# A transformer layer: the order of values and sums, more sevens in feed-forward 1, and gated results turned by transposing transfers

## The chip, the core and the metric

The kernel runs on one core of a Trainium2 chip. A core has a matrix engine (TensorE, PE in the profile; its weight loads are PEld), a vector engine (VectorE, DVE), a scalar engine (ScalarE, ACT), GpSimd (POOL) and a queue engine (SyncE, SP). Each runs its own instructions in order and waits for the others by semaphores. TensorE writes to PSUM, eight banks of 128 x 512 words; everything else lies in SBUF or in HBM. Transfers are issued from SP's or ScalarE's queue and are carried by 16 DMA engines. The metric is the device time of one execution in microseconds; less is better.

## The reference

One layer over 256 tokens of width 2048, in float32: a half feed-forward (SwiGLU, 5632 wide), two token mixers side by side (retention and sliding-window attention), a second half feed-forward, a gated input embedding, with a layer norm after each.

```python
def swiglu(x, w_gu, w_down):
    g, u = jnp.split(x @ w_gu, 2, axis=-1)
    return (jax.nn.silu(g) * u) @ w_down
...
h = layer_norm(alpha * h + 0.5 * swiglu(h, w_ffn1_gu[i], w_ffn1_down[i]), ln_g[i, 0], ln_b[i, 0])
rq, rk, rv, rg, aq, ak, av, gate_r, gate_a = jnp.split(h @ w_in[i], SPLIT_POINTS, axis=-1)
...
h = layer_norm(alpha * h + mixed, ln_g[i, 1], ln_b[i, 1])
h = layer_norm(alpha * h + 0.5 * swiglu(h, w_ffn2_gu[i], w_ffn2_down[i]), ln_g[i, 2], ln_b[i, 2])
```

The weights are random normal numbers, all different, so nothing can be left out.

## The kernel before

**Three matmuls for one.** A float32 product is made of parts in a format that TensorE takes at full pace: each operand is split into a high part (a cast on ScalarE, line 98) and a low part (a subtraction on VectorE, line 99), and three of the four products are added up (lines 374 to 376). Every weight is split on the way in, so each 512 KB chunk of weights costs a ScalarE cast and a VectorE subtraction of 128 x 1024 elements.

**Plain units and sevens.** Weight chunks come in pairs: two contraction blocks of 128 by two column blocks, against two blocks of 128 tokens. A plain unit ("P") multiplies all eight products, 24 matmuls, and needs two casts and two subtractions. A seven ("S", class `Seven`) has seven products (21 matmuls) after Strassen and Winograd; VectorE makes four sums of the weights for it (t1 to t4, lines 170 to 173, in tiles u and v), and ScalarE and VectorE split three more tiles. Its products go into the usual sums and into four banks of their own, which `seven_common` folds after the last seven of a block (lines 479 to 483). A "D" (`Prepared`) is a seven whose sums were made earlier, during the mixers, by `sums_ahead`, put away in HBM and loaded back.

**Feed-forward.** `ffn` runs 11 gate-up blocks (512 columns of gate and of up at a time), each a list of units from `gu_units`: block 0 all plain; in feed-forward 1 then "PPSPSPSP" in odd blocks and "PPSSPSSP" in even ones; in feed-forward 2 blocks 1 to 5 and 7 hold D units besides. After a block VectorE adds the sums (line 970), ScalarE takes Silu (line 971), VectorE multiplies (line 972), and the result v is turned (tokens by features to features by tokens) by eight transposes of 128 x 128 on TensorE into two banks and two copies on ScalarE (`turned`, lines 905 to 916). The down projection follows, in two halves.

**Order by hand.** Nothing is reordered: each engine's program is the order in which the Python code calls it. `plan` lists all weight units in the order of use. After each unit, `done` calls `fill`, which makes further units (casts, sums, subtractions) while those made ahead hold less than `ahead` matmul times (45; a plain chunk counts 12, a seven 21) and loads further ones while less than `far` (90) is under way and the slots suffice (`slots_for_weights`; 46 slots of 4 KB per partition in all). Then `run_side` runs one job of the list `side`; `later(n, job)` puts a job behind n others. It also takes a step of `lazy`, where `sums_ahead` and the rotary tables wait. PSUM banks and slots are handed out at the first write, those free longest first.

In steady state a gate-up block "PPSSPSSP" gives this order of making: first the next seven, then (after two units) the second seven, two plain chunks, the third and the fourth seven, four plain chunks, then the fold. `turned` runs behind the third chunk of the next block, that is between the second seven's casts and the next plain chunk's cast on ScalarE.

**The value projection.** `mixers` starts with the value block 0 (plain, its first part interleaved with the norm before), then splits it and makes the token forms that sevens need (`forms_of`), then runs value blocks 1 and 2 as one block of units "PSPSPSPS" (`VALUE_UNITS`, tiles rvsa, rvsb, rvss), then block 3 (plain, tile rv), then the rotary features (`features_out`, tile rqk).

Of the kernel before, what the change touches and what calls it, by code (L numbers as in the profile page):

```python
# [9 lines left out]
F32R = mybir.dt.float32r  # L10
I32 = mybir.dt.int32
AF = mybir.ActivationFunctionType
ALU = mybir.AluOpType
PSUM = bass.MemoryType.PSUM

P = 128
# [39 lines left out]
def layer(ctx: ExitStack, tc: tile.TileContext, io):  # L56
# [10 lines left out]
    def bank(name):  # L67
        return psum.tile([P, 512], F32, tag="ps", name=name)
# [4 lines left out]
    def slot(shape, dt, name):  # L73
        return slots.tile(shape, dt, tag="slot", name=name)
# [72 lines left out]
    class Seven:  # L147
# [12 lines left out]
        def make(self):  # L160
            a, b = self.a, self.b
            nm = a.name
            b11, b21, b12, b22 = a.of(a.raw, 0), a.of(a.raw, 1), b.of(b.raw, 0), b.of(b.raw, 1)
            u, v = (slot([P, 2, 512], F32, w + nm) for w in "uv")

            def shaped(x):
                return x.rearrange("p (g n) -> p g n", g=2) if a.paired else x

            t1, t3, t2, t4 = (shaped(x) for x in (u[:, 0], u[:, 1], v[:, 0], v[:, 1]))
            dve.tensor_tensor(t1, b11, b12, ALU.add)  # L170
            dve.tensor_tensor(t3, b12, b22, ALU.add)  # L171
            dve.tensor_tensor(t2, b11, t3, ALU.add)
            dve.tensor_tensor(t4, t2, b21, ALU.add)  # L173

            def parted(name, x):
                hi, lo = (slot([P, 2, 512], F32R, w + name + nm) for w in "hl")
                split(hi, lo, x)
                return [(hi[:, e], lo[:, e]) for e in range(2)]

            a.make()  # L180
            self.b11, self.b21 = a.columns(0), a.columns(1)
            both = slot([P, 2, 512], F32R, "b" + nm)
            self.b22 = both[:, 0], both[:, 1]
            split(shaped(both[:, 0]), shaped(both[:, 1]), b22)
            self.t1, self.t3 = parted("u", u)
            self.t2, self.t4 = parted("v", v)

# [215 lines left out]

    def block(name, units, keys, lhs, forms, sums, fold, before=None):


        sevens = [p for kind, p in units if kind != "P"]
        if sevens:
            p1, p6, p7, q5 = (Sum(bank(f"{name}s{j}"), len(sevens)) for j in range(4))
        for j, (kind, p) in enumerate(units):  # L410
# [24 lines left out]
            if p == sevens[-1]:  # L435
                fold(p1.ap, p6.ap, p7.ap, q5.ap)

    def seven_forms(full, hi, lo):
# [457 lines left out]
    def ffn(name, i, ht, norm, keep, residual, keepers, away):  # L896
# [9 lines left out]
        def turned(j, v):  # L906

            raw = slot([P, 4, S], F32, f"{name}a{j}")
            raws.append(raw)
            ps = banks(f"{name}t{j}")  # L910
            for k in range(4):
                for t in range(2):
                    at = slice(k % 2 * S + t * P, k % 2 * S + t * P + P)
                    pe.transpose(ps[k // 2][:, at], v[:, t, k * P : (k + 1) * P], ident)
            for h in range(2):
                act.copy(raw[:, 2 * h : 2 * h + 2], ps[h].rearrange("p (b n) -> p b n", b=2))

# [6 lines left out]

        for j in range(KF // 4):
            pg, pu = banks(f"{name}g{j}"), banks(f"{name}u{j}")
            units = gu_units(name, j)
# [36 lines left out]

            block(f"{name}{j}", units, gu_keys(name, j), rhs, forms, sums, lambda *a: got.extend(seven_common(*a)), before)
            if got:
# [148 lines left out]
    def mixers(ht, norm, residual, keepers, away):  # L1115
# [8 lines left out]

        rv = []
        made = {}
# [12 lines left out]
        def values(blk, ps):  # L1139
            hi, lo = (slot([P, 2, 512], F32R, f"rv{w}{blk}") for w in "hl")  # L1140
            if isinstance(ps, list):
                for t in range(2):
                    split(hi[:, t], lo[:, t], ps[t])
            else:
                split(hi, lo, ps)
            rv.append((hi, lo))

# [656 lines left out]
```

## Time and profile before

| | |
|---|---|
| three runs, median (lowest to highest) | 2283.04 us (2282.73 to 2283.24) |
| span of the profiled execution | 2282.8 us |
| feed-forward 1, ten gate-up blocks from turn to turn | 420.4 us |
| feed-forward 2, the same | 413.6 us |
| granted TensorE clock, mean | 0.996 |
| HBM read, written | 484.43 MB, 29.36 MB |

The span runs from the first to the last instruction of one profiled execution; it agrees with the runs. In views of instructions in order of time, a row gives start, duration, engine, line of the code, operation, output<-input and shapes, and in square brackets the idle time ahead of it with what ended it. VectorE's and ScalarE's instructions overlap a little, so the step from one start to the next is what an operation costs its engine. "PE 42.38 (x193)" in a stretch means busy time and number of instructions.

### The profile page before, as it was taken

To read this page: it belongs to the slowest core of one execution; us is meant where nothing else is said; L and a number is where in the kernel's file an instruction comes from. 1 tells how busy PE (TensorE), PEld (TensorE's weight loads), DVE (VectorE), ACT (ScalarE), POOL (GpSimd) and SP (SyncE) were. 2 spreads that over 40 slices of the span, in tenths; PEclk is the share of its full clock that TensorE was granted. 3 is DMA by queue.
4 is the path that set the end of the run, shared out by engine and by line. 5 is a ranking of instruction groups with operands and counts; after the bars stand their busy time and mean duration, and the time that the engine had idled before them with its cause. 6 is when DMAs were issued, how large, how long until landed. Compare 5 with 4: busy or idle time off the path is not lost.

```text
span 2282.8 us, 29225 instructions
## 1 busy us (share of the span) xinstructions
PE 2265.0 (99%) x10485; PEld 1881.8 (82%) x10485; DVE 2025.6 (89%) x2628; ACT 1233.5 (54%) x1502; POOL 2.3 (0%) x9
## 2 busy tenths in 40 slices
PE   9999999999999899999999999999999999999999
PEld 7888888888887788888778888888888888888887
DVE  7999999999989989888789788789999999889887
ACT  6555555556554545445565545455555565655543
POOL 0000000000000000000000000000000000000000
PEclk9999999999999899999999999999999999999999
DMA  8666665665677679876446658886867766555872
GB/s 300 208 199 200 198 208 180 207 198 183 228 278 255 220 251 298 283 231 213 152 143 202 225 179 290 305 287 223 291 240 255 263 203 207 199 186 211 290 272 74
DMA packets 211129, 515.72 MB, mean 226 GB/s; under 512 B 16412, under 2 KB 20892, under 8 KB 210984
## 3 DMA queue, kind: packets, MB, share of 16 engines
q1 hardware_dynamic: 209000, 511.28, 66.2%
q10 hardware_dynamic: 1984, 2.58, 0.4%
q8 instruction: 82, 1.34, 0.2%
q14 instruction: 63, 0.52, 0.1%
HBM read 484.43 MB, written 29.36 MB: 225 GB/s over the span
## 4 chain that ended last, share of the span: by engine, by line
PE 97%; DVE 1%; DMA 1%; ACT 0%; issue 0%; ACTq 0%; SPq 0%; DVEq 0%
PE f1g L374 3%; PE f1g L376 3%; PE f1g L375 3%; PE f2g L376 3%; PE f2g L375 3%; PE f2g L374 3%; PE rqk L325 3%; PE f1u L374 2%; PE f1u L375 2%; PE f1u L376 2%; PE f2u L375 2%; PE f2u L376 2%; PE f2u L374 2%; PE aqk L325 2%; PE f2d L374 2%; PE f1d L376 2%
## 5 line engine op out<-in xcount | busy, mean ns | idle before, releaser
L99 DVE TENSOR_TENSOR lf_gu<-rf_gu,hf_gu 128x1024 fp32r<-128x1024 f32 (+1 forms) x274 | 323.2, 1211 | 13.9 <-ACT hf_gu L98 12.8
L98 ACT CAST hf_gu<-rf_gu 128x1024 fp32r<-128x1024 f32 (+1 forms) x274 | 273.9, 1043 | 29.9 <-DMA rf_gu<-in_f_gu 27.5
L99 DVE TENSOR_TENSOR lf_down<-rf_down,hf_down 128x1024 fp32r<-128x1024 f32 x150 | 178.7, 1220 | 16.8 <-ACT hf_down L98 16.3
L99 DVE TENSOR_TENSOR lw_in_f<-rw_in_f,hw_in_f 128x1024 fp32r<-128x1024 f32 x140 | 167.6, 1220 | 24.7 <-ACT hw_in_f L98 24.6
L98 ACT CAST hf_down<-rf_down 128x1024 fp32r<-128x1024 f32 x150 | 151.7, 1050 | 48.7 <-DMA rf_down<-in_f_down 20.4
L98 ACT CAST huf_gu<-uf_gu 128x1024 fp32r<-128x1024 f32 x70 | 73.8, 1054 | 145.6 <-DVE uf_gu L171 135.1
L98 ACT CAST hw_in_f<-rw_in_f 128x1024 fp32r<-128x1024 f32 x140 | 140.6, 1050 | 8.7 <-PE rqk L333 2.3
L374 PE MATMUL f1g<-hf_gu,xt 128*128 128x512 f32 x247 | 96.4, 390 | 0.5 <-ACT hf_gu L98 0.5
L376 PE MATMUL f1g<-lf_gu,xt 128*128 128x512 f32 x247 | 96.5, 391 | 0.0
L375 PE MATMUL f1g<-hf_gu,xt 128*128 128x512 f32 x247 | 96.2, 389 | 0.0
L98 ACT CAST hvf_gu<-vf_gu 128x1024 fp32r<-128x1024 f32 x70 | 73.8, 1054 | 29.5 <-DVE vf_gu L173 29.0
L971 ACT ACTIVATE eve<-eve 128x1024 f32<-128x1024 f32 x20 | 21.2, 1062 | 126.7 <-DVE eve L970 126.7
L99 DVE TENSOR_TENSOR luf_gu<-uf_gu,huf_gu 128x1024 fp32r<-128x1024 f32 x70 | 85.3, 1219 | 0.0
L99 DVE TENSOR_TENSOR lvf_gu<-vf_gu,hvf_gu 128x1024 fp32r<-128x1024 f32 x70 | 85.3, 1219 | 0.0
L374 PE MATMUL f2g<-hf_gu,ht 128*128 128x512 f32 x217 | 84.7, 390 | 0.0
L376 PE MATMUL f2g<-lf_gu,ht 128*128 128x512 f32 x217 | 84.7, 390 | 0.0
L375 PE MATMUL f2g<-hf_gu,ht 128*128 128x512 f32 x217 | 84.5, 389 | 0.0
L374 PE MATMUL f1u<-hf_gu,xt 128*128 128x512 f32 x212 | 83.4, 394 | 0.0
L375 PE MATMUL f1u<-hf_gu,xt 128*128 128x512 f32 x212 | 82.6, 390 | 0.0
L376 PE MATMUL f1u<-lf_gu,xt 128*128 128x512 f32 x212 | 82.6, 390 | 0.0
L374 PE MATMUL f2u<-hf_gu,ht 128*128 128x512 f32 x172 | 68.2, 397 | 0.0
L376 PE MATMUL f2u<-lf_gu,ht 128*128 128x512 f32 x172 | 67.1, 390 | 0.0
(1562 smaller groups left out, 6606.4 us busy)
## 6 DMA issues: line engine op xcount, KB each, us to landing
rf_gu<-in_f_gu SPq DMA_DIRECT2D x360, 512.0 KB
rf_down<-in_f_down SPq DMA_DIRECT2D x176, 512.0 KB
rw_in_f<-in_w_in_f SPq DMA_DIRECT2D x148, 512.0 KB
rw_rv<-in_w_rv SPq DMA_DIRECT2D x32, 512.0 KB
rw_ret<-in_w_ret SPq DMA_DIRECT2D x32, 512.0 KB
rw_mix<-in_w_mix SPq DMA_DIRECT2D x32, 512.0 KB
rw_pg<-in_w_pg SPq DMA_DIRECT2D x32, 512.0 KB
rw_att<-in_w_att SPq DMA_DIRECT2D x16, 512.0 KB
```

The costliest lines, as they stand in the source:

```text
L98: act.copy(dst_hi, src)
L99: (lo_engine or dve).tensor_tensor(dst_lo, src, dst_hi, ALU.subtract)
L325: pe.matmul(ps[f], hi[:, kk, f * P : (f + 1) * P], rhs(k), start=k == 0, stop=k == n_k - 1,)
L374: pe.matmul(o, al, bh, start=first, stop=False)
L375: pe.matmul(o, ah, bh, start=False, stop=False)
L376: pe.matmul(o, ah, bl, start=False, stop=self.left == 0)
L971: act.activation(g, g, AF.Silu)
```

## The change

Four things are edited. (1) In `Seven.make`, the order of the casts, sums and subtractions: sum three is made first, sum four after the low part of the first chunk; the work is the same. (2) In `mixers` and the plan, value block 3 comes before blocks 1 and 2. (3) `gu_units` gives every block without D units "PPSSPSSP": five more sevens in feed-forward 1 and one (block 9) in feed-forward 2. (4) `turned` no longer uses TensorE: ScalarE copies the upper and lower 16-bit halves of v into a tile `parts`, a transposing transfer of 16-bit words goes from ScalarE's queue to a tile `turns`, and three jobs later `join` copies the halves back together (two ScalarE copies). The product of gate and up is put off by one job, and from block 2 on, every other block names its four seven banks before its gate and up banks.

```diff
             t1, t3, t2, t4 = (shaped(x) for x in (u[:, 0], u[:, 1], v[:, 0], v[:, 1]))
+            a.make_hi()
...
+            act.copy(a.hi, a.raw)
+            act.copy(h22, b22)
+            dve.tensor_tensor(t3, b12, b22, ALU.add)
             dve.tensor_tensor(t1, b11, b12, ALU.add)
-            dve.tensor_tensor(t3, b12, b22, ALU.add)
             dve.tensor_tensor(t2, b11, t3, ALU.add)
+            act.copy(uh, u)
+            dve.tensor_tensor(a.lo, a.raw, a.hi, ALU.subtract)
             dve.tensor_tensor(t4, t2, b21, ALU.add)
...
+            act.copy(vh, v)
+            dve.tensor_tensor(l22, b22, h22, ALU.subtract)
+            dve.tensor_tensor(ul, u, uh, ALU.subtract)
+            dve.tensor_tensor(vl, v, vh, ALU.subtract)
...
-    def block(name, units, keys, lhs, forms, sums, fold, before=None):
+    def block(name, units, keys, lhs, forms, sums, fold, before=None, extra=None):
...
-            p1, p6, p7, q5 = (Sum(bank(f"{name}s{j}"), len(sevens)) for j in range(4))
+            p1, p6, p7, q5 = (Sum(b, len(sevens)) for b in extra or seven_banks(name))
...
-        order = "PPSSPSSP" if j % 2 == 0 else "PPSPSPSP"
-        return units_of(order, SEVEN[: order.count("S")])
+        return units_of("PPSSPSSP", SEVEN)
...
         def turned(j, v):
 
+            parts = slot([P, 2, 2, 512], U16, f"{name}w{j}")
+            words = v.bitcast(U16).rearrange("p t (n w) -> p w t n", w=2)
+            for w in range(2):
+                act.copy(parts[:, w], words[:, w])
+            turns = slot([P, 16, P], U16, f"{name}t{j}")
+            act.dma_start_transpose(turns, parts.rearrange("p w t n -> p (w t n)"))
+            later(3, lambda: join(j, turns))
+
+        def join(j, turns):
             raw = slot([P, 4, S], F32, f"{name}a{j}")
             raws.append(raw)
-            ps = banks(f"{name}t{j}")
-            for k in range(4):
-                for t in range(2):
-                    at = slice(k % 2 * S + t * P, k % 2 * S + t * P + P)
-                    pe.transpose(ps[k // 2][:, at], v[:, t, k * P : (k + 1) * P], ident)
-            for h in range(2):
-                act.copy(raw[:, 2 * h : 2 * h + 2], ps[h].rearrange("p (b n) -> p b n", b=2))
+            words = raw.bitcast(U16).rearrange("p k (t n w) -> p w k t n", t=2, w=2)
+            turns = turns.rearrange("p (w t k) n -> p w k t n", w=2, t=2)
+            for w in range(2):
+                act.copy(words[:, w], turns[:, w])
...
+            extra = seven_banks(f"{name}{j}") if j and j % 2 == 0 else None
             pg, pu = banks(f"{name}g{j}"), banks(f"{name}u{j}")
...
-                dve.tensor_tensor(v, g, v, ALU.mult)
+                later(1, lambda g=g, v=v: dve.tensor_tensor(v, g, v, ALU.mult))
...
         plan_tokens(("w_rv", 0), KD)
+        plan_tokens(("w_rv", 3), KD)
         block_units(VALUE_UNITS, value_keys)
-        plan_tokens(("w_rv", 3), KD)
...
+        ps = banks("rv3")
+        tokens_out(("w_rv", 3), KD, rhs, ps)
+        values(3, ps)
+        slots_for_weights(22)
         for n, v in enumerate(mixer_block("rvs", VALUE_UNITS, value_keys, rhs)):
             values(1 + n, v)
         made.clear()
         slots_for_weights(14)
-        ps = banks("rv3")
-        tokens_out(("w_rv", 3), KD, rhs, ps)
-        values(3, ps)
```

More of the change, by code (lines that the diff above doesn't have):

```diff
@@ L11 @@
 I32 = mybir.dt.int32
+U16 = mybir.dt.uint16
 AF = mybir.ActivationFunctionType
@@ L169, in make @@
             t1, t3, t2, t4 = (shaped(x) for x in (u[:, 0], u[:, 1], v[:, 0], v[:, 1]))
+            a.make_hi()
+            both = slot([P, 2, 512], F32R, "b" + nm)
+            h22, l22 = shaped(both[:, 0]), shaped(both[:, 1])
+            uh, ul, vh, vl = (slot([P, 2, 512], F32R, w + nm) for w in ("hu", "lu", "hv", "lv"))
+            act.copy(a.hi, a.raw)
+            act.copy(h22, b22)
+            dve.tensor_tensor(t3, b12, b22, ALU.add)
             dve.tensor_tensor(t1, b11, b12, ALU.add)
-            dve.tensor_tensor(t3, b12, b22, ALU.add)
             dve.tensor_tensor(t2, b11, t3, ALU.add)
+            act.copy(uh, u)
+            dve.tensor_tensor(a.lo, a.raw, a.hi, ALU.subtract)
             dve.tensor_tensor(t4, t2, b21, ALU.add)
[L175 to L180, printed above, removed]
+            act.copy(vh, v)
+            dve.tensor_tensor(l22, b22, h22, ALU.subtract)
+            dve.tensor_tensor(ul, u, uh, ALU.subtract)
+            dve.tensor_tensor(vl, v, vh, ALU.subtract)
             self.b11, self.b21 = a.columns(0), a.columns(1)
-            both = slot([P, 2, 512], F32R, "b" + nm)
             self.b22 = both[:, 0], both[:, 1]
-            split(shaped(both[:, 0]), shaped(both[:, 1]), b22)
-            self.t1, self.t3 = parted("u", u)
-            self.t2, self.t4 = parted("v", v)
+            self.t1, self.t3 = ((uh[:, e], ul[:, e]) for e in range(2))
+            self.t2, self.t4 = ((vh[:, e], vl[:, e]) for e in range(2))
     put_by_sums = {}
@@ L436, in block, with seven_banks @@
                 fold(p1.ap, p6.ap, p7.ap, q5.ap)
+    def seven_banks(name):
+        return [bank(f"{name}s{j}") for j in range(4)]
     def seven_forms(full, hi, lo):
@@ L963, in before @@
                     convert(u // 2 - 2)
-            block(f"{name}{j}", units, gu_keys(name, j), rhs, forms, sums, lambda *a: got.extend(seven_common(*a)), before)
+            block(f"{name}{j}", units, gu_keys(name, j), rhs, forms, sums, lambda *a: got.extend(seven_common(*a)), before, extra)
             if got:
@@ L1145, in values @@
                 split(hi, lo, ps)
[L1146 removed]
+            rv[blk] = hi, lo
         ps = banks("rv0")
```

2 lines of the change are left out of this document (1 added, 1 removed).

## The prediction

> **What bounds the kernel now.** I read the page first, then the stretches of the two gate-up loops, then who waits for whom, then VectorE's and ScalarE's instructions in order of time.
>
> ```profile
> span 2282.8 us, 29225 instructions
> PE 2265.0 (99%) x10485; PEld 1881.8 (82%) x10485; DVE 2025.6 (89%) x2628; ACT 1233.5 (54%) x1502; POOL 2.3 (0%) x9
> ```
>
> TensorE is idle for 17.8 us in all, so a gain must be matmul time taken away or one of its few waits. VectorE at 89% is close behind, which asks for a look at the stage.
>
> ```profile
> 58.25:100.63 42.38, 42.38 (x193) 35.19 (x192) 37.39 (x44) 23.43 (x27) 0.00 (x0) 1.00 0.69 222
> 100.63:142.33 41.70, 41.70 (x190) 34.64 (x189) 41.11 (x50) 23.98 (x27) 0.00 (x0) 1.00 0.60 191
> ...
> sum 420.40, PE 420.40 PEld 349.21 DVE 395.88 ACT 238.11 POOL 0.00; mean PE 42.04 PEld 34.92 DVE 39.59 ACT 23.81 POOL 0.00
> ```
>
> These stretches run from one turn of feed-forward 1 to the next (length; busy of PE, PEld, DVE, ACT, POOL; granted clock; DMA share; GB/s). The first is a block with three sevens, the second one with four, and so on in turn: ten blocks in 420.4 us, TensorE never idle. With four sevens VectorE is busy 41.11 of 41.70; only the blocks of three leave it 5 us. The ten like stretches of feed-forward 2:
>
> ```profile
> sum 413.60, PE 413.60 PEld 343.56 DVE 389.99 ACT 234.49 POOL 0.00; mean PE 41.36 PEld 34.36 DVE 39.00 ACT 23.45 POOL 0.00
> ```
>
> TensorE's long waits stand in the value projection:
>
> ```profile
> PE rvsa L374 <- DVE rvf0l L99: 6.5, 1, 6.5
> PE rv L374 <- DVE evw L480: 3.3, 1, 3.3
> ```
>
> **What TensorE saves.** From the chain of waits, the eight transposes of one turn:
>
> ```profile
> 58.25 0.87 PE f1t L914 x8
> ...
> 100.63 0.87 PE f1t L914 x8
> ```
>
> 22 turns of 0.87 make 19.1 us: twenty inside the stretches, two in the first down blocks (1.7 us). One seven in a pair of plain units' place is worth 42.38 - 41.70 = 0.68 us. Five more come in feed-forward 1 and one in block 9 of feed-forward 2 (its order is chosen by the same edited line): 6 x 0.68 = 4.1 us. A block of four sevens then needs 41.70 - 0.87 = **40.83 us** of TensorE, and an average block of feed-forward 1 now takes 42.04.
>
> **What VectorE's cycle becomes.** VectorE in block 2, where it has no gap:
>
> ```profile
> 101.10 0.69 DVE L170 TENSOR_TENSOR uf_gu<-rf_gu,rf_gu 128x512 f32<-128x512 f32 x1
> 101.70 0.69 DVE L171 TENSOR_TENSOR uf_gu<-rf_gu 128x512 f32<-128x512 f32 x1
> 102.42 0.69 DVE L172 TENSOR_TENSOR vf_gu<-rf_gu,uf_gu 128x512 f32<-128x512 f32 x1
> 103.15 0.69 DVE L173 TENSOR_TENSOR vf_gu<-vf_gu,rf_gu 128x512 f32<-128x512 f32 x1
> 103.76 1.22 DVE L99 TENSOR_TENSOR lf_gu<-rf_gu,hf_gu 128x1024 fp32r<-128x1024 f32 x1
> ...
> 106.63 1.22 DVE L99 TENSOR_TENSOR lvf_gu<-vf_gu,hvf_gu 128x1024 fp32r<-128x1024 f32 x1
> 107.77 2.35 DVE L99 TENSOR_TENSOR lf_gu<-rf_gu,hf_gu 128x1024 fp32r<-128x1024 f32 x2
> ...
> 130.10 0.68 DVE L483 TENSOR_TENSOR evw<-f12s,eve 128x512 f32<-128x512 f32 x1
> ...
> 142.21 1.22 DVE L99 TENSOR_TENSOR lvf_gu<-vf_gu,hvf_gu 128x1024 fp32r<-128x1024 f32 x1
> ```
>
> A seven takes eight operations, 101.10 to 107.77: 6.67 us. Its last one starts at 106.63; the same one three sevens, eight plain chunks and a fold later starts at 142.21. A block of four sevens thus costs VectorE 35.58 + 6.67 = **42.25 us**, against 41.70 on TensorE. It falls behind in such a block and catches up in the next.
>
> The new order inside a seven helps. An add that needs the result just before it starts 0.72 after it (101.70 to 102.42, 102.42 to 103.15), one that does not 0.61 (103.15 to 103.76). Sums one and three are swapped and a 1.13 us subtraction (106.63 to 107.77) stands ahead of the fourth sum, so both bubbles go: about 0.27 us a seven, 4 x 0.27 = 1.1 a block. Putting the product off by one unit saves the 0.1 to 0.2 us in which it waits for Silu. VectorE's cycle falls to about **41.0 us**. In the other stages' sevens the same 0.27 lies behind TensorE and is worth nothing.
>
> 41.0 against 40.83 would be a tie, if ScalarE were not in the way. Its instructions at the turn:
>
> ```profile
> 103.93 1.06 ACT L98 CAST hvf_gu<-vf_gu 128x1024 fp32r<-128x1024 f32 x1 [0.40 <-DVE vf_gu L173]
> 104.89 1.06 ACT L916 COPY f1a<-f1t 128x512 f32<-128x512 f32 x2
> 105.84 2.95 ACT L98 CAST hf_gu<-rf_gu 128x1024 fp32r<-128x1024 f32 x3
> ...
> 811.24 0.35 ACTq L818 DMA_DIRECT2D pos_ia<-in_positions  x1
> ```
>
> The turn stands between the casts of the second seven and the cast of the next plain chunk, and the first of those waits for the fourth sum on VectorE. Now the two copies (0.95 together) fit: the chunk's cast starts at 105.84 and is done at 106.9, 0.9 us before VectorE asks for it at 107.77. After the change ScalarE does there two copies of 1024 half words (I take 0.95 each, the step from 103.93 to 104.89), drains them, and issues the transfer. Counted from the fourth sum's end (3.69 us into the seven's 6.4): cast 1.05, copies 1.9, 0.2 for draining and semaphores, issue, chunk's cast 1.05. With the 0.35 us of a plain issue the cast is done at 8.3, and VectorE, ready at 6.4, stands still for 1.9 us. At the join two more copies (1.9) stand after the fourth seven's casts: done at 7.7, a stall of 1.3. Neither stall is made good, since VectorE has nothing left over: that such a cast can hold it shows already, in the rare cases where it comes late.
>
> ```profile
> DVE lf_gu L99 <- ACT hf_gu L98: 12.8, 18, 1.3
> ```
>
> The issue of a transposing transfer is in no row. Its lower bound is the 0.35 above; its upper bound is 16 of them, one for each 128 columns of the source: 5.6 us. It is one instruction on the same queue, so I go near the low end and take **1.0 us**. VectorE's cycle is then 41.0 + 1.9 + 1.3 + 0.65 = 44.85; I take **44.7 us**, since the drain may lie inside the issue.
>
> [...]
>
> Feed-forward 1: 10 x (44.7 - 40.83) = 38.7 us behind. Some is covered: the fold's last operation ended at 130.8 (row of 130.10), the next block's first matmul, which takes those banks, came 36 matmuls of 0.227 (0.68 / 3) before the turn at 142.33, at 134.2: 3.4 us, say 4 with what is made ahead. So 408.3 + 34.7 = 443 us, **+22.6**. Feed-forward 2 has cheaper blocks: where a prepared seven replaces one (1.73 us of VectorE for 6.4), the cycle is 39.5 us in three-seven blocks, 44.2 in the others, against 40.15 on TensorE. The short blocks and the cover of 4 take up most of what blocks 2, 4 and 6 lose; blocks 8 to 10 lose up to 3.9 each. I take 13 in all: 413.6 - 10 x 0.87 - 0.68 + 13 = 417.2, **+4**. So the gate-up loops lose more than TensorE saves in them. Each tenth of a us in the stall is worth 1.6 us of the time (ten blocks and some six).
>
> **The join's wait.** The join comes four units after the turn: two plain chunks and two sevens of VectorE's work, 2.3 + 12.8 = 15 us. A load of the same 512 KB took:
>
> ```profile
> 716.87 7.97 DMA rw_rv<-in_w_rv
> ```
>
> So I cost landing at nothing; beyond 15 us each us would hold ScalarE, and through it both engines, in every block. [...]
>
> **The values.** The first wait is real time, and more than itself:
>
> ```profile
> 746.18 0.80 PE L374 MATMUL rvsa<-bw_rv,rvf0l 128*128 128x512 f32 x1 [6.48 <-DVE rvf0l L99]
> ...
> 751.89 0.40 PE L375 MATMUL rvsb<-hvw_rv,ht 128*128 128x512 f32 x1
> ```
>
> Behind it 13 matmuls take 5.71 us, where 13 x 0.227 = 2.95 are due: TensorE runs at half pace at first. 6.5 + 2.8 = 9.3 us. Behind the second wait likewise: 3.3 + 2.8 = 6.1.
>
> ```profile
> 730.84 0.69 DVE L170 TENSOR_TENSOR uw_rv<-rw_rv,rw_rv 128x512 f32<-128x512 f32 x1
> ...
> 737.51 2.35 DVE L99 TENSOR_TENSOR lw_rv<-rw_rv,hw_rv 128x1024 fp32r<-128x1024 f32 x2
> ...
> 750.03 1.23 DVE L99 TENSOR_TENSOR rvf1l<-sums,rvf1h 128x1024 fp32r<-128x1024 f32 x1 [1.11 <-ACT rvf1h L98]
> ```
>
> With block 3 first, plain chunks are made from 730.84 on in place of a seven (6.67), the forms are done some 4 us earlier, about 747. The wait opened at 746.18 - 6.48 = 739.7, 30 matmuls after block 0's end, which was at 732.9. From there TensorE now has six of block 3's chunks, made by the planner's look-ahead, which last 16.3 us; it needs the seventh at 749.2. The first wait goes: **-9.3** (bounds 0, if a wait of its size opens there, and -15.4, if both go). The second I keep at its size: the fold of the sevens now stands before the first rotary features, VectorE's work up to it is the same but for 1 us, and the next features take the banks that the fold frees. The eight loads of block 3 move ahead of the sevens' on SP's queue; all have room there.
>
> **Edits at nothing.** Banks: the sums' banks came free 3.4 us before the next block used them, so their order changes nothing; were the gate's banks taken instead, each block would start 1 to 2 us late. Two more buffers per turn out of 46, and 0.5 MB per turn at a DMA share of 0.6 to 0.7: hidden behind loads that run ahead; without that cover the loads come late by the transfer's 2 to 8 us.
>
> **Sum**: +22.6 + 4 - 1.7 - 9.3 = +15.6 on the profiled 2282.8 (0.2 below the median of the runs): **2299 us**.
>
> **Rivals.** *TensorE stays the bound* (faster). If ScalarE's casts are not late, all savings stand: -19.1 - 4.1 - 9.3 = -32.5, **2250**. For it: VectorE's 41.0 ties with 40.83, and the averages leave VectorE 24.5 us in feed-forward 1. Against: those 24.5 lie in the three-seven blocks, which go. It is full where a block's stalls are nothing; by 1.6 us a tenth, the kernel is faster than before from stalls of 2.7 us downward (a cycle of 43.7), slower above. *ScalarE is held long by the issue*: at 2.8 us, eight plain issues, 1.8 more in some 16 bound blocks, +29: **2328**. For it: one instruction turns 16 column groups; against: the plain issue took a third of a us. [...] *Loss and gain cancel*, **2283**: at that cycle of 43.7, and a plain issue of 0.35 gives 44.0, which is near.
>
> **Chances.** Forecast 0.45 (its own range 2286 to 2318), TensorE-bound 0.27, long hold 0.20, cancelling 0.08. The range 2248 to 2338 leaves out the worst holds. A difference under 0.2% (4.6 us) can't be told from none: faster 0.28, within 0.09, slower 0.63.
>
> **What would show it.** Stretches of feed-forward 1 of 44 to 45 us with TensorE idle 3 to 4 us in each, and VectorE waiting for ScalarE's cast after the second and fourth seven; the first value wait gone, one before the rotary features. Stretches of 40.8 us would prove me wrong, ones beyond 46 the hold; waits of ScalarE for the transfer would show a late landing.

## The result, and the profile after

The changed kernel takes **2366.59 us** (median of 4 runs, 2364.87 to 2368.96) against 2282.99 us (2282.73 to 2283.24): a ratio of 1.0365, 95% interval 1.0353 to 1.0378. It is slower by 84 us. 2299 us was predicted, in a range up to 2338: the sign was right, and the loss is more than five times the 15.6 us forecast. Lines of the code behind `split` have moved: 99 and 100 are its cast and subtraction now, 175 to 186 the seven, 378 to 380 the matmuls, 917 to 928 the turn.

The page's head and its row of the queue that ScalarE issues on (packets, MB, share of the DMA engines), which held 1984 packets and 2.58 MB before:

```profile
span 2367.1 us, 28892 instructions
PE 2290.3 (97%) x10291; PEld 1873.1 (79%) x10291; DVE 2029.5 (86%) x2664; ACT 1312.1 (55%) x1558; POOL 2.3 (0%) x9
...
q10 hardware_dynamic: 47744, 14.11, 3.5%
```

TensorE runs 194 instructions fewer than before (22 turns of eight, and three matmuls for each of six sevens) and is nevertheless busy for 25 us more, and idle for 77 us where it was idle for 18. VectorE's work has hardly grown (2025.6 us before). ScalarE is busy for 79 us more (copies; the page does not count issues of transfers as busy time, so they come on top), and its queue has new traffic: 45,760 packets for 22 transfers of 0.5 MB. The stages say where. Each is measured from its first matmul to the first matmul of the next, as the views by tile give them; for the two down projections, in the changed kernel:

```profile
L378 PE MATMUL f1d<-hf_down,f1al x141: 387/389/628, 516.4 to 637.8; 128*128 128x512 f32 x141
...
L378 PE MATMUL f2d<-hf_down,f2al x141: 389/389/628, 2029.3 to 2149.4; 128*128 128x512 f32 x141
```

| stage, us | before | after | difference |
|---|---|---|---|
| feed-forward 1, gate-up (first matmul to 516.4) | 465.4 | 511.0 | +45.6 |
| its first down block | 117.2 | 122.1 | +4.9 |
| values (to the rotary features) | 102.4 | 88.1 | -14.3 |
| rotary features | 89.4 | 95.2 | +5.8 |
| feed-forward 2, gate-up (to 2029.3) | 460.0 | 498.7 | +38.7 |
| its first down block | 117.2 | 120.8 | +3.6 |

All else differs by 0.6 us at most. So the gate-up loops lost 84 us by themselves; the 8.5 us that the values gained are lost again in the down blocks. Stretches of feed-forward 1, from one transposing transfer's issue to the next (length; busy of PE, PEld, DVE, ACT, POOL; granted clock; DMA share; GB/s):

```profile
65.80:111.86 46.06, 44.65 (x196) 36.32 (x195) 41.02 (x49) 27.73 (x30) 0.00 (x0) 1.00 0.66 202
...
157.33:205.97 48.64, 44.06 (x182) 34.85 (x181) 41.02 (x49) 27.74 (x30) 0.00 (x0) 0.93 0.69 184
...
301.43:347.24 45.81, 42.33 (x182) 33.46 (x181) 41.03 (x49) 27.75 (x30) 0.00 (x0) 1.00 0.65 196
...
sum 464.40, PE 429.87 PEld 341.99 DVE 405.10 ACT 276.21 POOL 0.00; mean PE 42.99 PEld 34.20 DVE 40.51 ACT 27.62 POOL 0.00
```

VectorE's work is 41.02 us in every block of four sevens, which was forecast as 41.0; what varies is the rest: 5.0, 7.6 and 4.8 us of idle time in these three. Now the turn at the start of the second of them, on ScalarE and on VectorE (start, duration, engine, line, what; in brackets the idle time ahead and what ended it):

```profile
154.35 1.06 ACT L183 CAST hvf_gu<-vf_gu 128x1024 fp32r<-128x1024 f32 x1 [1.29 <-DVE vf_gu L182]
155.31 1.99 ACT L917 COPY f1w<-evw 128x1024 uint16<-128x1024 uint16 x2
157.33 4.45 ACTq L919 DMA_TRANSPOSE f1t<-f1w  x1
161.87 1.99 ACT L99 CAST hf_gu<-rf_gu 128x1024 fp32r<-128x1024 f32 x2 [4.58 <-issue]
```

```profile
155.92 1.21 DVE L186 TENSOR_TENSOR lvf_gu<-vf_gu,hvf_gu 128x1024 fp32r<-128x1024 f32 x1
162.95 2.36 DVE L100 TENSOR_TENSOR lf_gu<-rf_gu,hf_gu 128x1024 fp32r<-128x1024 f32 x2 [5.82 <-ACT hf_gu L99]
...
179.80 4.63 DVE L100 TENSOR_TENSOR lf_gu<-rf_gu,hf_gu 128x1024 fp32r<-128x1024 f32 x4 [1.66 <-ACT hf_gu L99]
```

The third ScalarE row is new: the issue itself keeps ScalarE for 4.45 us. The cast behind it, which has nothing to do with the transfer, starts at 161.87, and VectorE, which was through at 157.1, stands still until that cast is done. The second stall, 1.66 us at 179.80, follows the join's two copies. The views by tile give all issues and the join's copies (duration in ns: shortest/median/longest; first and last start):

```profile
L919 ACTq DMA_TRANSPOSE f1t<-f1w x11: 1332/3177/4449, 65.8 to 530.2; - x11
...
L928 ACT COPY f1a<-f1t x22: 1329/1346/1363, 82.2 to 544.0; 128x1024 uint16<-128x1024 uint16 x22
...
L919 ACTq DMA_TRANSPOSE f2t<-f2w x11: 1334/3142/8005, 1587.0 to 2043.1; - x11
```

Issues of 1.3 to 8.0 us. Set against VectorE's idle time (length less its work), stretch by stretch, they account for feed-forward 1:

| stretch from | issue, us | VectorE idle, us | idle less issue |
|---|---|---|---|
| 65.80 | 1.93 | 5.04 | 3.1 |
| 111.86 | 1.33 | 4.45 | 3.1 |
| 157.33 | 4.45 | 7.62 | 3.2 |
| 205.97 | 3.27 | 6.44 | 3.2 |
| 253.44 | 3.91 | 6.97 | 3.1 |
| 301.43 | 1.33 | 4.78 | 3.4 |
| 347.24 | 4.00 | 7.13 | 3.1 |
| 395.39 | 1.94 | 5.06 | 3.1 |
| 441.47 | 3.29 | 6.45 | 3.2 |

In these blocks every us of an issue is a us of the block, and 3.1 to 3.4 us come on top of it whatever its length. The view of waits has the same thing in sum, where before there were 18 such waits with 12.8 us:

```profile
DVE lf_gu L100 <- ACT hf_gu L99: 110.8, 49, 7.6
```

TensorE feels it at second hand. In the groups of its instructions (count | busy us, mean ns | idle before, what ended it), the matmuls of feed-forward 1 that wait are also slower, 417 ns against 390 before, with granted clocks of 0.93 to 0.96 in seven of the nine stretches; and the values' second wait has moved, as forecast:

```profile
L378 PE MATMUL f1g<-hf_gu,xt 128*128 128x512 f32 x232 | 96.8, 417 | 23.6 <-ACT hf_gu L99 23.6
...
L329 PE MATMUL rqk<-ht,hw_in_f 128*128 128x512 f32 x256 | 66.6, 402 | 2.8 <-DVE evw L487 2.8
```

### The profile page after: what moved, and what is told of

Its sections match the earlier page's. It is cut to its first block, busy times and chain, and to the rows that moved or that the text cites. A ratio compares the mean times of both kernels' runs of the same rounds, so it can differ in the third digit from the quotient of the medians.

```text
span 2367.1 us, 28892 instructions
## 1 busy us (share of the span) xinstructions
PE 2290.3 (97%) x10291; PEld 1873.1 (79%) x10291; DVE 2029.5 (86%) x2664; ACT 1312.1 (55%) x1558; POOL 2.3 (0%) x9
## 3 DMA queue, kind: packets, MB, share of 16 engines
q8 instruction: 81, 1.33, 0.2%
## 4 chain that ended last, share of the span: by engine, by line
PE 76%; DVE 12%; issue 4%; ACT 3%; ACTq 3%; DMA 2%; DVEq 0%; SPq 0%; POOL 0%; POOLq 0%
ACTq L919 3%; PE rqk L329 3%; DVE lf_gu L100 2%; PE f1g L380 2%; PE f2g L380 2%; PE f2g L378 2%; PE f2g L379 2%; PE f1g L378 2%; PE f1g L379 2%; PE aqk L329 2%; PE f2u L378 1%; PE f2u L380 1%; PE f2u L379 1%; PE rqk L337 1%; PE f2e L380 1%
## 5 line engine op out<-in xcount | busy, mean ns | idle before, releaser
L100 DVE TENSOR_TENSOR lf_gu<-rf_gu,hf_gu 128x1024 fp32r<-128x1024 f32 (+1 forms) x192 | 223.8, 1209 | 111.8 <-ACT hf_gu L99 110.8
L99 ACT CAST hf_gu<-rf_gu 128x1024 fp32r<-128x1024 f32 (+1 forms) x192 | 189.9, 1038 | 67.5 <-issue 43.2
L100 DVE TENSOR_TENSOR lw_in_f<-rw_in_f,hw_in_f 128x1024 fp32r<-128x1024 f32 x132 | 157.9, 1219 | 25.9 <-ACT hw_in_f L99 25.8
L100 DVE TENSOR_TENSOR lf_down<-rf_down,hf_down 128x1024 fp32r<-128x1024 f32 x124 | 147.1, 1220 | 27.1 <-ACT hf_down L99 25.9
L99 ACT CAST hf_down<-rf_down 128x1024 fp32r<-128x1024 f32 x124 | 125.1, 1048 | 34.6 <-DMA rf_down<-in_f_down 14.7
L99 ACT CAST hw_in_f<-rw_in_f 128x1024 fp32r<-128x1024 f32 x132 | 132.7, 1050 | 9.6 <-DMA rw_in_f<-in_w_in_f 2.7
L181 DVE TENSOR_TENSOR lf_gu<-rf_gu,hf_gu 128x1024 fp32r<-128x1024 f32 x76 | 92.5, 1217 | 19.3 <-ACT hf_gu L175 19.3
L175 ACT CAST hf_gu<-rf_gu 128x1024 fp32r<-128x1024 f32 x76 | 79.2, 1042 | 21.2 <-DMA lvf_gu<-lvdf_gu 8.1
L378 PEld LDWEIGHTS f1g<-hf_gu,xt 128*128 128x128 f32 x232 | 46.7, 201 | 36.6 <-ACT hf_gu L99 27.4
L378 PE MATMUL f1u<-hf_gu,xt 128*128 128x512 f32 x192 | 75.1, 391 | 0.0
L379 PE MATMUL f1u<-hf_gu,xt 128*128 128x512 f32 x192 | 74.8, 389 | 0.0
```

What stands on the lines that cost most here:

```text
L99: act.copy(dst_hi, src)
L100: (lo_engine or dve).tensor_tensor(dst_lo, src, dst_hi, ALU.subtract)
L175: act.copy(a.hi, a.raw)
L181: dve.tensor_tensor(a.lo, a.raw, a.hi, ALU.subtract)
L378: pe.matmul(o, al, bh, start=first, stop=False)
L379: pe.matmul(o, ah, bh, start=False, stop=False)
```

## The experiments

The theory after this reading: the issue holds ScalarE for its whole length and the half-word copies add 3.1 us; both delay casts, and VectorE, which has no time to spare in blocks of four sevens, hands the delay on. Rivals: the extra sevens overfill VectorE by themselves; the copies are enough; the transfers disturb the loads or land late; the banks. All ratios are to the kernel before, run beside it.

**TensorE's turns again and the banks in their old order, all else as changed.**

```diff
-            parts = slot([P, 2, 2, 512], U16, f"{name}w{j}")
...
+            ps = banks(f"{name}t{j}")
+            for k in range(4):
+                for t in range(2):
+                    at = slice(k % 2 * S + t * P, k % 2 * S + t * P + P)
+                    pe.transpose(ps[k // 2][:, at], v[:, t, k * P : (k + 1) * P], ident)
+            for h in range(2):
+                act.copy(raw[:, 2 * h : 2 * h + 2], ps[h].rearrange("p (b n) -> p b n", b=2))
...
-            extra = seven_banks(f"{name}{j}") if j and j % 2 == 0 else None
+            extra = None
```

> The changed kernel with the turn given back to TensorE (eight transposes, two PSUM banks, two copies on ScalarE) and the banks in their old order; the values' order, the order inside a seven and the four sevens in every block stay. Theory (the transfer's issue and its copies hold ScalarE, and VectorE waits for its casts): without them VectorE's cycle of 41.0 us lies under TensorE's 41.70 (the four-seven stretch of before), so ten blocks take 417 to 418 us, feed-forward 2 gains 0.7, the value stage 8.5: about 2270 us, 2266 to 2276. Rival (the extra sevens alone overfill VectorE): stretches of 42.25 us and more, so no gain in feed-forward 1 and a loss of some 2 to 20 us there: 2277 to 2295.

2278.52 us, ratio 0.9981 (0.9971 to 0.999). The loss is gone, so the sevens do not make it; but 8 us of the expected gain were missing. The chain of TensorE's turns shows where:

```profile
100.32 1.07 PE L920 MATMUL f1t<-ident,evw 128*128 128x128 f32 x8 [0.26 <-DVE evw L979]
142.50 1.06 PE L920 MATMUL f1t<-ident,evw 128*128 128x128 f32 x8 [0.26 <-DVE evw L979]
```

Stretches of 42.18 us, with a wait for the product (line 979) ahead of each turn: the change computes that product one job later, and TensorE's turns, unlike ScalarE's copies, reach it too early.

**The same with the product at once.**

```diff
-                later(1, lambda g=g, v=v: dve.tensor_tensor(v, g, v, ALU.mult))
+                dve.tensor_tensor(v, g, v, ALU.mult)
```

> The first run's kernel (turns on TensorE, old banks, all the rest of the change) with the product of a gate's result computed at once again and not one unit later. Theory: in that run each turn of TensorE waited 0.26 us for the late product and a stretch took 42.16 us where 41.70 were due; without it ten blocks of feed-forward 1 take 417 to 418, feed-forward 2 413: 19 turns of 0.46 us less, about 2270 us, 2267 to 2274. Rival (the four sevens in every block cost the 0.46 us): 2277 to 2280, no change against the first run.

2269.88 us, ratio 0.9941 (0.9926 to 0.9957): this version is faster than both kernels. Its stretches of feed-forward 1:

```profile
99.76:141.45 41.69, 41.69 (x189) 34.61 (x188) 41.20 (x50) 24.35 (x29) 0.00 (x0) 1.00 0.62 200
...
sum 417.00, PE 417.00 PEld 346.15 DVE 411.39 ACT 244.73 POOL 0.00; mean PE 41.70 PEld 34.62 DVE 41.14 ACT 24.47 POOL 0.00
```

With the new order inside the sevens, VectorE carries four of them in every block (41.2 of 41.7 us) and TensorE is never idle: 417.0 in place of 420.4, five times 0.68.

**The transposing transfers alone.** The kernel before with `turned` and `join` of the changed one, nothing else.

> The kernel before with the transposing transfers alone: three and four sevens by turns, the old order inside a seven, the old order of the values, the old banks. Theory (hold of ScalarE): in the changed kernel VectorE stood idle 3.2 us plus the issue in each block; the same six us a block here, on a VectorE cycle of 42.25 us with four sevens and some 38 with three, so about 48.3 and 44 us: feed-forward 1 loses some 30 to 40 us, feed-forward 2 some 35 to 45, the first down blocks 8: about 2360 us, 2340 to 2375. Rival (the sevens are at fault): TensorE's saving of 19 us shows, 2264 to 2285.

2336.85 us, ratio 1.0239 (1.0223 to 1.0254), a little under the range. Feed-forward 2 loses the full 38.7 us (498.7), but feed-forward 1 only 12.0 (477.4 against 465.4): its blocks of three sevens, with 5 us to spare on VectorE, take up more than I had counted. Shorter issues are not the reason: its ten sum to 27.8 us, against 26.8 in the changed kernel. The parts do not add up: sevens and their order alone give -3.9 us in feed-forward 1 (461.5, the version above), the transfers alone +12.0, both together +45.6.

**Three sevens again in odd blocks.**

```diff
-        return units_of("PPSSPSSP", SEVEN)
+        order = "PPSSPSSP" if j % 2 == 0 else "PPSPSPSP"
+        return units_of(order, SEVEN[: order.count("S")])
```

> The changed kernel with three sevens again in the odd blocks of feed-forward 1 and in block 9 of feed-forward 2. Theory (VectorE is full, so each us of its work in these stages is a us of the time): a seven less frees 6.4 us of VectorE and adds four plain chunk parts of 1.15 us each at most, so an odd block falls from some 47 us to about 43: 5 x 4 = 20 us in feed-forward 1 and up to 4 in feed-forward 2: about 2344 us, 2336 to 2352. Rival (TensorE's slow clock behind its waits is what costs, VectorE is not the bound): TensorE's extra 0.68 us a block, so no gain: 2364 to 2372.

2350.96 us, ratio 1.0307 (1.0275 to 1.034): 16 us less than the changed kernel, all in feed-forward 1 (493.6 against 511.0), 3.5 us for each seven taken out, although the ten issues there sum to 33.8 us in place of 26.8. That fits VectorE as the bound; TensorE alone would have lost 0.68 us a block.

**The transfer left out.** The copies stay, so the results are not turned; every other instruction is there.

```diff
-            turns = slot([P, 16, P], U16, f"{name}t{j}")
-            act.dma_start_transpose(turns, parts.rearrange("p w t n -> p (w t n)"))
+            turns = parts.rearrange("p w t (k n) -> p (w t k) n", k=4)
```

> The changed kernel without the transposing transfer itself: the two copies of half words at the turn and the two at the join stay, and the join reads the words that the first two copies wrote (so the results are not turned). Theory: VectorE's idle time in a block of feed-forward 1 was 3.2 us plus that block's issue, so what goes is the issues: 26.8 us in ten blocks, some 30 of 40.9 in feed-forward 2 (a part of them lies behind its lighter blocks), some 6 in the first down blocks. About 2304 us, 2296 to 2314, stretches of feed-forward 1 near 44.1 us with VectorE idle for some 3.1 us in each. Rival (the copies and their place, not the issue): over 2340. Rival (the issue alone): all of the loss goes, 2250 to 2265.

2295.98 us, ratio 1.0059 (1.0043 to 1.0076): 71 us of the loss go with the transfer; the time is just below the expected range. Feed-forward 1 falls by 28.4 us to 482.6, for 26.8 us of issues, feed-forward 2 by 35.4 to 463.3, for 40.9. VectorE's two stalls that are left in a block:

```profile
109.70 2.36 DVE L100 TENSOR_TENSOR lf_gu<-rf_gu,hf_gu 128x1024 fp32r<-128x1024 f32 x2 [1.15 <-ACT hf_gu L99]
126.55 4.63 DVE L100 TENSOR_TENSOR lf_gu<-rf_gu,hf_gu 128x1024 fp32r<-128x1024 f32 x4 [1.66 <-ACT hf_gu L99]
```

1.15 us at the turn's copies, 1.66 at the join's. The four half-word copies a block, even without the transfer, leave feed-forward 1 21.1 us behind the version with TensorE's turns (482.6 against 461.5), though those turns take 8.7 us of TensorE there. The two kernels also differ in the place of the product and in the banks.

**The transfer issued on SP's queue.**

```diff
-            act.dma_start_transpose(turns, parts.rearrange("p w t n -> p (w t n)"))
+            sync.dma_start_transpose(turns, parts.rearrange("p w t n -> p (w t n)"))
```

> The changed kernel with the transposing transfer issued on SP's queue, among the weight loads, and not on ScalarE's; the copies stay on ScalarE. Theory (the issue holds the engine that issues it): as without the transfer, about 2306 us, 2296 to 2316, the issue of 1.3 to 8 us now in SP's queue with no engine waiting for it. Rival (the transfers in flight, or their landing, delay the work wherever they are issued): stays above 2340, with ScalarE waiting at the join, or VectorE and ScalarE waiting for weight loads.

2313.85 us, ratio 1.0138 (1.0123 to 1.0153). The same transfers fly and land, and 53 us of the loss are gone, so it is the issuing engine that pays. Feed-forward 1 is at 485.4, near the run without transfers. The issues are also shorter on this queue:

```profile
L919 SPq DMA_TRANSPOSE f1t<-f1w x11: 1322/1929/2892, 65.3 to 503.4; - x11
```

SP comes to them after a wait, and in 21 of the 22 the DMA engines are at most 42% busy meanwhile. Feed-forward 2 keeps 479.2, 16 us above the run without transfers, and the waits say why. SP stands at the issue until the copies are done: the largest group of its waits has 13 of them, 202 us in all. The weight loads behind it in the queue go out late, and VectorE waits for them:

```profile
SPq L919 <- ACT hf_gu L99: 201.9, 13, 22.4
```

```profile
DVE uf_gu L177 <- DMA rf_gu<-in_f_gu: 16.8, 6, 7.7
```

**That, and the copies on GpSimd.**

```diff
-                act.copy(parts[:, w], words[:, w])
+                pool.tensor_copy(parts[:, w], words[:, w])
...
-                act.copy(words[:, w], turns[:, w])
+                pool.tensor_copy(words[:, w], turns[:, w])
```

> The changed kernel with the transposing transfer on SP's queue, as in the run before this, and all four copies of a turn on GpSimd, which does nothing else in these stages: ScalarE has no part in the turn any more. Theory: the copies hold VectorE's casts for the 3.1 us a block that were left without the transfer; with them gone VectorE's cycle is 41.0 us against TensorE's 40.86, so feed-forward 1 falls from 485 us to about 458, feed-forward 2 loses its share of the copies (some 10 of 479) but keeps the waits for weight loads behind SP's waiting queue: about 2275 us, 2258 to 2285. Rival (copies of half words on GpSimd slow VectorE down, or come so late that the join is awaited): VectorE's mean times rise from 1.22 and 0.69 us, or waits for GpSimd show; above 2300.

2466.4 us, ratio 1.0803 (1.0784 to 1.0823): the rival, and worse. GpSimd, SP and VectorE in order of time:

```profile
102.19 16.79 POOL L917 COPY f1w<-evw 128x1024 uint16<-128x1024 uint16 x2 [12.66 <-PE f1u L380]
123.40 2.56 POOL L928 COPY f1a<-f1t 128x1024 uint16<-128x1024 uint16 x2 [4.42 <-issue]
```

```profile
119.00 1.90 SPq L919 DMA_TRANSPOSE f1t<-f1w  x1
```

```profile
115.87 1.22 DVE L186 TENSOR_TENSOR lvf_gu<-vf_gu,hvf_gu 128x1024 fp32r<-128x1024 f32 x1
```

Two copies that take ScalarE 2.0 us take GpSimd 16.8. From 100.76 to 117.1 VectorE worked without a gap; GpSimd was done 1.9 us after it stopped, so its two copies lasted over more than fifteen VectorE instructions. Over all turns, one such copy takes between 1.04 and 16.9 us, so the copy is not slow in itself; what held GpSimd beside a busy VectorE, no view shows. SP waited for these copies, in both feed-forwards together 413 us, and VectorE for the weight loads behind SP:

```profile
SPq L919 <- POOL f1w L917: 222.6, 11, 27.1
SPq L919 <- POOL f2w L917: 190.4, 11, 22.0
```

```profile
DVE uf_gu L177 <- DMA rf_gu<-in_f_gu: 165.1, 15, 12.1
```

The join's copies tell the landing: they began 4.4 us after the issue began (119.00 to 123.40), the landing included.

**The old order of the banks.**

```diff
-            extra = seven_banks(f"{name}{j}") if j and j % 2 == 0 else None
+            extra = None
```

> The changed kernel without the alternation of the accumulator banks: each block takes the banks of gate and up again, which the adds behind the fold free. Theory (VectorE is the bound through ScalarE's casts, and TensorE waits for it anyway): TensorE begins each block 1 to 2 us later, which lies in its waiting time: 2366 to 2378 us. Rival (the alternation carries weight of its own): every block late by some 3 us, 18 late blocks, beyond 2400.

2367.62 us, ratio 1.0372 (1.0353 to 1.039): no difference from the changed kernel that can be told from none. This fits a later start of TensorE in time in which it waits anyway.

**The values' order alone.** Kernel before, edit (2) of the change only.

> The kernel before with the values' order alone: block 3 straight behind block 0, the sevens of blocks 1 and 2 behind it. Theory (the wait of 6.5 us and the half pace behind it go, the wait for the fold only moves to the rotary features, with some 3 to 6 us of its own): 8.5 to 11.3 us less, as the stages from the first value matmul to the retention gate showed in the runs so far: about 2273 us, 2270 to 2276. Rival (the gain hung on the shorter sevens): 2276 to 2283.

2275.21 us, ratio 0.9969 (0.9957 to 0.998): 7.6 us. From the first value matmul to the retention gate 184.5 us instead of 191.8.

**The order inside a seven alone.** Kernel before, edit (1) only.

> The kernel before with the new order inside a seven alone. Theory: VectorE saves 0.27 us a seven, but in the kernel before it makes good in each three-seven block what it lacks in a four-seven one, and TensorE is never idle: nothing, 2281 to 2285, stretches of feed-forward 1 still 42.38 and 41.70. Rival (the saving reaches the end of each block): 1.1 us a block, 2265 to 2278.

2281.07 us, ratio 0.9994 (0.9986 to 1.0003): within what can be told from nothing. In its profile the values take 3.8 us less (98.6 against 102.4) and the gate-up loops hardly change (464.8 and 459.9). By itself the order is worth little or nothing, though VectorE's busy time falls from 2025.6 to 2008.0 us; the version with four sevens everywhere needs it, by this reading, since 42.25 us of VectorE would not have fitted there. That kernel, more sevens in the old order, was not run.

**The issue by itself, whole and half.** The fastest version, plus a transfer behind the turn's copies into a tile that nobody reads.

```diff
+            unread = slot([P, 16, P], U16, f"{name}w{j}")
+            act.dma_start_transpose(unread, v.bitcast(U16).rearrange("p t n -> p (t n)"))
```

> The fastest kernel so far (turns on TensorE) with a transposing transfer of the same size issued on ScalarE's queue behind the turn's two copies, into a tile that nobody reads: the issue by itself, without half words copied and without a join. Theory: cast 1.05, copies 0.95, the issue, cast 1.05 from 3.7 us into the seven, VectorE ready at 6.4: it stands still for about the issue plus 0.3; with 1.3 to 8 us, mean near 3 in feed-forward 1 and 4 in feed-forward 2, a cycle of 44.2 us against 41.70, some 20 us in each feed-forward: about 2312 us, 2295 to 2330. Rival (the issue costs nothing without the copies): 2269 to 2276.

2283.23 us, ratio 1.0001 (0.9992 to 1.001): 13 us over the fastest version, a third of what was expected. On ScalarE (line 924 is this transfer) and on VectorE:

```profile
107.16 1.33 ACTq L924 DMA_TRANSPOSE f1w<-evw  x1
...
231.97 3.86 ACTq L924 DMA_TRANSPOSE f1w<-evw  x1
```

```profile
110.04 2.36 DVE L100 TENSOR_TENSOR lf_gu<-rf_gu,hf_gu 128x1024 fp32r<-128x1024 f32 x2 [0.22 <-ACT hf_gu L99]
...
237.01 2.36 DVE L100 TENSOR_TENSOR lf_gu<-rf_gu,hf_gu 128x1024 fp32r<-128x1024 f32 x2 [2.38 <-ACT hf_gu L99]
```

In these two turns VectorE waits the issue less 1.1 to 1.5 us, where I had put the issue plus 0.3: with only 0.95 us of copies ahead of it, the first 1.1 to 1.5 us of an issue pass before VectorE needs the next cast, and the blocks have 0.5 us left. In the changed kernel the half-word copies fill that gap. Now half the words:

```diff
+            unread = slot([P, 8, P], U16, f"{name}w{j}")
+            act.dma_start_transpose(unread, v.bitcast(U16)[:, 0])
```

> As the run before this, with half the words (128x1024 in place of 128x2048). Theory (the issue's time goes with the number of descriptors that it writes): shortest issue near 0.7 us, middle one near 1.6, so VectorE stands still for some 1.9 us and has 0.7 to spare: about 2283 us, 2275 to 2296. Rival (a fixed time, whatever the size): the same times and the same total as with the full size.

```profile
L924 ACTq DMA_TRANSPOSE f1w<-evw x10: 1247/1249/1262, 103.8 to 476.0; - x10
```

2271.52 us, ratio 0.9955 (0.994 to 0.997): neither theory. The issue of half the words is 1.25 us every time, almost the 1.33 of the shortest whole one, and never longer than 1.33. So the time is not in proportion to the size, and holds like those of the whole words in the run before (up to 5.69 us) did not appear with a half alone.

**Two halves, together and apart.** The changed kernel with two transfers of 128x1024, first one behind the other, then the second with its copy one job later.

```diff
-            act.dma_start_transpose(turns, parts.rearrange("p w t n -> p (w t n)"))
+            for w in range(2):
+                act.dma_start_transpose(turns[:, 8 * w : 8 * w + 8], parts[:, w].rearrange("p t n -> p (t n)"))
```

> The changed kernel with the transposing transfer as two of half the size, one behind the other on ScalarE's queue. Theory (a half holds ScalarE for 1.25 us and never longer, as in the run with half the words): 2.5 us a turn, always, in place of 26.8 us in the ten turns of feed-forward 1 and 40.9 in those of feed-forward 2; 2 us less in the first, some 12 less in the second: about 2352 us, 2345 to 2358. Rival (what fills up is the queue, by words and not by instructions, so the second half waits as the whole does): second halves of 1.25 to 7 us, 2362 to 2378.

> The changed kernel with two transfers of half the size, the first with its copy at the old place, the second with its copy one step of work later. Theory (each half 1.25 us): the same 2.5 us and the same copies in two places: 2345 to 2360. Rival of the full queue: here too the first half has been taken by the time the second is issued, so both short, 2345 to 2360, while the run before this one stays above 2362; if this one stays above 2362 as well, the long holds do not go with the size of one issue.

2357.71 us, ratio 1.0328 (1.0312 to 1.0344) together, and 2336.83 us, ratio 1.0229 (1.0212 to 1.0246) apart. The issues of feed-forward 2, together and then apart:

```profile
L920 ACTq DMA_TRANSPOSE f2t<-f2w x22: 1248/1324/7460, 1579.6 to 2032.2; - x22
```

```profile
L920 ACTq DMA_TRANSPOSE f2t<-f2w x22: 1247/1249/2257, 1568.7 to 2023.3; - x22
```

Together, each first half takes 1.25 to 1.64 us and the second is held, for up to 7.5 us, as the rival had it. The total fell inside the theory's range all the same: feed-forward 1 is 6.6 us shorter than in the changed kernel (504.4), though its ten turns' issues sum to more (30.1 us). The first half needs only the first copy, and its issue runs beside the second one: at the second turn the copies run from 108.99 to 110.98, and the first issue starts at 110.06. One step apart, none runs over 2.3 us and nearly all take 1.25; 2336.83 us is below the expected range. So on ScalarE's queue the hold of a half went with what was put there just before: up to 7.5 us behind another half, at most 2.3 us one step apart.

In the changed kernel its length also went with how busy the DMA engines were. Two issues of the changed kernel, as stretches (length, busy times, clock, DMA share, GB/s):

```profile
301.43:302.76 1.33, 1.33 (x7) 0.82 (x5) 0.00 (x0) 0.00 (x0) 0.00 (x0) 1.00 0.28 26
...
1763.03:1771.04 8.01, 6.04 (x27) 4.68 (x25) 1.43 (x3) 0.00 (x0) 0.00 (x0) 1.00 1.01 277
```

All fourteen of its issues over 2.1 us fall where the DMA engines are 73% busy or more, and six of the eight shorter ones where they are at most 59% busy. Halves apart are different: 42 of 44 take at most 1.4 us, whether the DMA engines are nearly idle (2%) or fully busy. The transfer's own traffic is part of the share, and no run changed the loads alone, so what sets the length stays open.

## Why the prediction was right on the side and wrong on the size

**Where it failed: the issue.** "It is one instruction on the same queue, so I go near the low end and take 1.0 us." It measured 1.3 to 8.0 us, 2.7 on average over the ten turns of feed-forward 1 (26.8 / 10) and 4.1 over those of feed-forward 2. The bounds of 0.35 and 5.6 us were bounds for a fixed size times a count, and the issue fits neither: the shortest ones took 1.25 us for half the words and 1.33 for all of them, the longest one 6.7 us more. 1.7 us a block too little in the first stage and 3.1 in the second make up to 48 of the 69 us that were missing (84.3 - 15.6). By stage, 23.0 us were missing in feed-forward 1, 34.7 in feed-forward 2 and 10.2 in the down blocks. The rival "held long by the issue" named the place, but with 2.8 us and 16 bound blocks it, too, stopped at 2328.

**Feed-forward 2: +4 was forecast, +38.7 came.** Beside the longer issues, the forecast let its short blocks and prepared sevens cover most of the hold. Without the transfer the stage takes 463.3 us, 3.3 above before, and 35.4 us of the loss go with 40.9 us of issues. A tenth of a us was said to be worth 1.6 us; the two stages together give 63.8 us for 67.7 us of issues in twenty blocks, 1.9 a tenth.

**The down blocks** were credited with TensorE's 1.7 us and lost 8.5: the last turn and join of each feed-forward fall in them and hold casts of the down weights. VectorE's waits for these casts grew from 16.3 to 25.9 us. This was overlooked.

**Right: VectorE's cycle.** 41.0 us forecast without stalls, 41.02 us of work measured; the four-seven block fits TensorE's 41.70 (the fastest version). TensorE's stretch of 40.83 without its turns was never seen, since something else was always slower.

**Right, with a small error: the copies.** Forecast 1.55 us at the turn without its issue and 1.3 at the join; measured 1.37 (5.82 - 4.45) and 1.66 in the turn shown above, 1.15 and 1.66 without the transfer. The join's copies, 1.35 us each, were taken as 0.95, like copies of words. The 0.2 us for draining and semaphores in that sum is shown by no run: in the turn shown above 0.03 us lie between the copies' end and the issue (157.30 to 157.33), and 0.09 us between the issue's end and the cast (161.78 to 161.87).

**Right: the landing.** Costed at nothing; no wait of ScalarE for it appears in the changed kernel. From the start of the issue to the join took 4.4 us on SP's queue, below the 7.97 us of a plain load.

**Right: the values.** -9.3 forecast, -8.5 in the changed kernel (up to -11.4 in the profiles of other versions with this order and the new sevens), -7.6 alone. The first wait is gone and the second stands ahead of the rotary features (2.8 us) with its slow stretch, which only some of the versions show.

**Right: the banks** are worth nothing. **Wrong in a detail: the product.** Put off, it was said to save 0.1 to 0.2 us; with TensorE's turns it cost 0.48 us a block. In the changed kernel it was not tried by itself.

## What to carry to other kernels

An issue was work of the engine whose queue it stood in (1.3 to 8.0 us on ScalarE's): before putting a transfer there, look at what that engine owes next, and to whom. A place with slack swallowed the first 1.1 to 1.5 us of a hold (the issue by itself) and handed on the rest. Filling another engine to the brim (here VectorE, by more sevens) removes the slack that made the delay harmless, so that in feed-forward 1 edits that cost -4 and +12 us apart cost +46 together. Moving the wait to another queue, or another engine, moved the question there (one group of VectorE's waits for weight loads behind SP: 16.8 us with the copies on ScalarE, 165.1 us with them on GpSimd): ask what stands behind it.

## What the runs showed of the hardware

The issue of a transposing transfer of 512 KB held ScalarE for 1.3 to 8.0 us in the changed kernel and for up to 9.7 us in the run with the old order of the banks; on SP's queue it took 1.3 to 2.9 us. One of 256 KB took 1.25 us nearly always (2.3 at most), unless another had been issued just before (up to 7.5 us). Long issues went with DMA engines that were 73% busy or more in the changed kernel.

A matmul of split parts, 128x128 by 128x512, came every 0.227 us at a granted clock of 1.00 in the kernel before; TensorE's eight float32 turns of 128x128 took 0.87 us there.

ScalarE's copy of 128x1024 half words took 1.04 us with a stride in what it reads (line 917) and 1.35 us with one in what it writes (line 928).

In one run, GpSimd's two copies at a turn took 16.8 us beside a busy VectorE, and its two copies at the join 2.6 us while VectorE stood still.

After the same wait of 2.8 us, the rotary features took between 92.4 and 95.3 us (first matmul to the retention gate's). With TensorE's turns and the late product (92.4) the granted clock stayed at 1.00 behind the wait; with the product at once (95.3) it was 0.50 for some 6 us. A difference of 3 us between kernels with that wait need not come from their edits.
